# Modulation product in two matmul passes with four columns, context tiles scaled on VectorE, and a new order ahead of the first projection

## The chip, the cores and the metric

One core of one Trainium2 chip runs the whole layer as one program. The metric is the device time of one execution in microseconds (us), lower is better; the time before is the median of three executions. In the text, PE is the matmul engine (TensorE) and PEld its weight load, DVE is VectorE, ACT is ScalarE, POOL is GpSimd, and SP (SyncE) issues most of the DMAs.

## The reference, cut to what matters

The layer takes 1024 latent tokens and 256 context tokens of width 1024. Two conditioning vectors, `c` for latent tokens and `c_ctx` for context tokens, go through a SiLU and one matrix `w_mod`; the first two blocks of 1024 columns of that product are a shift and a scale for the normalised tokens. Everything else follows from the projection of the tokens so modulated.

```python
sh1, sc1, gt1, sh2, sc2, gt2 = split(silu(c) @ w_mod + b_mod, 6)        # latent tokens
sh1c, sc1c, ...              = split(silu(c_ctx) @ w_mod + b_mod, 6)    # context tokens
p  = (rms_norm(x,  norm1_g) * (1 + sc1)  + sh1)  @ w_in
pc = (rms_norm(xc, norm1_g) * (1 + sc1c) + sh1c) @ w_in
# p, pc -> differential attention and a gated delta rule, side by side
# -> output projection -> mixture of experts -> final norm
```

All of it is float32, and the kernel keeps that precision by splitting each operand into a part that the matmul takes exactly (hi, type fp32r) and the rest (lo = operand - hi).

## The kernel before

**Stages.** The program runs through modulation (to about 44 us in the profile), the projection of value and decay columns token by token (`pvab`, about 44 to 80 us), the projection of the other columns, a mix stage in which the delta rule and the attention share the engines (about 505 to 930 us), the output projection and the experts. A list scheduler orders each engine's instructions once, when the program is built; blocks marked `high_priority` are pulled ahead. On the chip each engine then runs its own list strictly in that order, and so does each DMA queue.

**Modulation** (`_modulation`). `w_mod`'s 1024 rows are taken in eight tiles of 128 rows by 2048 columns (1 MB, `wm`, three buffers, loaded through SP at L532). Before that a small chain makes the conditioning columns: a transpose to PSUM (`pv`, L546), a copy (`vec`, L547), half of it (`xh`, L553), a tanh on ACT (`th`, L554), `cs` (L555), and its hi and lo parts `csh`, `csl`. Each `wm` tile is cut into four pieces j of 512 columns. For a piece, ACT copies the hi part (`wmh`, L175), VectorE subtracts it from the original (`wml`, L176; POOL does this for j = 3 of the first six tiles), and PE adds three matmuls to one PSUM row (`mm3`, L170 to L172): csh with hi, csl with hi, csh with lo. `wmh` and `wml` have four buffers each. Two pieces of the last tile are one float32 matmul each instead (L570). A tile's buffer is loaded again, with the tile three further on, when its four subtractions are done.

**Rows to columns.** When the eighth tile is in, the two PSUM rows (2 x 2048) are copied (`mrow`, L581 and L582), transposed to 128 partitions (`pmt`, L585), and the bias is added: `mod` and `modA` are the scale, `modB` the shift (L586 to L588).

**Tokens** (`_tokens`). The two context tiles of 128 tokens come first, then latent tokens in two groups of four tiles. Per tile ACT sums the squares (`junk`, L603), VectorE makes the reciprocal root (L606 and `nt`, L148 to L163), and the tile is scaled: on ACT for the context tiles (L612), on VectorE for the latent ones (L610). PE transposes (`px`, L617), ACT writes the hi part with scale and shift (`XH`, L621), VectorE the same unrounded (`xm`, L622) and then the rest (`XL`, L623).

**First projection** (`_inproj`). Its weights come as four loads `wvr` (L390, L391), of which the last two reuse `wm` buffers and so wait for the last tiles' subtractions, and are split into `wvh` (ACT) and `wvl` (VectorE or POOL). `K.after` (L117) writes one element of a buffer on POOL so that its load waits for a chosen value: the loads of the first six latent tiles wait for `mod` this way. The `pvab` matmuls are L170 to L172 again.

**Mix** (`_mix`). The delta rule is a generator of short steps (POOL masks, PE products `p_x` L812, `p_d` L819, `p_dt` L824, VectorE `QF` L820); after every few steps the attention, 32 units of one head and one block of 128 tokens, takes its turn: scores `sp` (L1038, L1039), row maximum `mx` (L1041), exponent `pt` (L1044), combination (L1051), transposes `ptr`, products with the values `po`.

Of the kernel before, what the change touches and what calls it, by code (L numbers as in the profile page):

```python
# [367 lines left out]
def _inproj(K, banks):  # L368
# [8 lines left out]
    with tc.tile_pool(name="p1v", bufs=1, reuse_waits="tile") as pv, \  # L377
# [3 lines left out]
        with tc.tile_pool(name="p0", bufs=1, reuse_waits="tile") as pe:  # L381
            with tc.tile_pool(name="p0m", bufs=1, space=PSUM, side="right", reuse_waits="tile") as psm:
                xts, *late, raws = _modulation(K, pe, ps0, psm)
            for j in range(4):
                if j < 2:
                    wr = pv.tile([P, 2, 528], F32, name="wvr", bufs=2)
                    K.after(wr[:, 0, 0:1], late[0])
                else:
                    wr = raws.pop(0)[:, :2 * 528].rearrange("p (k f) -> p k f", k=2)
                nc.sync.dma_start(wr[:, :, 0:512], w_in[:, 2 * j:2 * j + 2, 1024:1536])  # L390
                nc.sync.dma_start(wr[:, :, 512:528], w_in[:, 2 * j:2 * j + 2, 3584:3600])  # L391
                for i in range(2):
# [132 lines left out]
def _modulation(K, pe, ps, psm):  # L525
# [19 lines left out]
    pv = ps.tile([P, 512], F32, name="pv", tag="px", bufs=3)[:, :110]  # L545
    nc.tensor.transpose(pv, vr, ident[:110, :110])  # L546
    nc.vector.tensor_copy(K.vec, pv)  # L547
    vec = K.vec
    nc.vector.tensor_scalar(K.convw, vec[:, 72:109], 0.5, None, op0=ALU.mult)
# [3 lines left out]
    nc.vector.tensor_scalar(xh, vec[:, 0:16], 0.5, None, op0=ALU.mult)  # L553
    nc.scalar.activation(th, xh, AF.Tanh)  # L554
    nc.vector.scalar_tensor_tensor(K.cs, th, 1.0, xh, op0=ALU.add, op1=ALU.mult)  # L555
    csk = K.cs.rearrange("p (w k) -> p k w", w=2)
    csh, csl = (pe.tile([P, KT, 2], F32R, name=nm) for nm in ("csh", "csl"))
    K.split(csh, csl, csk)
    pm = psm.tile([2, 2048], F32, name="pmod")
    xts, los = {}, []  # L560
    for kt in range(KT):
# [31 lines left out]
def _tokens(K, pe, ps, xts, late):  # L593
# [3 lines left out]
    for t0, n in TOKEN_GROUPS:  # L597
# [1169 lines left out]
```

## Time and profile before

| | us |
|---|---|
| three executions | 1691.02, 1693.51, 1685.58 |
| their median | 1691.02 |
| the profiled execution | 1684.6 |
| its span | 1682.8 |

| engine | busy us | share of the span |
|---|---|---|
| PE | 1536.3 | 91% |
| PEld | 1296.7 | 77% |
| DVE | 1297.9 | 77% |
| ACT | 913.7 | 54% |
| POOL | 610.7 | 36% |

The span is the time between the first and the last record of the profiled execution; 1.8 us of its own time lie around it. PE is busy nearly throughout, except at the start and in a few stretches, so a stage must be read by its own rows: the share over the whole span says nothing of the first 44 us. A timeline row gives the start, the length, the engine, the line and tile of an instruction, and in brackets how long the engine had been idle before it and what ended the wait.

### The profile page before, as it was taken

The numbers are of one execution on the slowest core, as the hardware profiler recorded it, in microseconds if no ns is written. First come the engines' busy times: TensorE is split into PE (matmuls) and PEld (weight loads), VectorE is DVE, ScalarE is ACT, GpSimd is POOL, SyncE is SP. The second block draws the span as 40 slices with busy tenths as digits, with TensorE's granted clock in tenths as the row PEclk, the third lists the DMA queues.
The fourth block names the chain that finished last, engine by engine and source line by source line (L and its number), as shares of the span: only waits on it lengthen the run. The fifth ranks groups of instructions, "written<-read, shape, count | busy, mean of one in ns | idle before, by whom it ended". The sixth has DMA issues, their size and how long they took to land.

```text
span 1682.8 us, 24852 instructions
## 1 busy us (share of the span) xinstructions
PE 1536.3 (91%) x8805; PEld 1296.7 (77%) x8805; DVE 1297.9 (77%) x2081; ACT 913.7 (54%) x1512; POOL 610.7 (36%) x555
## 2 busy tenths in 40 slices
PE   6999889899986998989899899499999999999994
PEld 2898668788876998889798788378888887777872
DVE  6757655587768777878788743799999998999985
ACT  6521125344422655656466232387777877777873
POOL 3013331232225865383640021534455333341101
PEclk9999899999997999999999999699999999999997
DMA  7477953444546031322313494799999999999965
GB/s 267 172 234 231 287 143 114 129 135 131 177 150 203 21 96 57 118 75 101 92 47 127 143 316 154 275 362 360 399 399 397 383 397 374 384 384 382 378 224 187
DMA packets 171280, 378.76 MB, mean 225 GB/s; under 512 B 32590, under 2 KB 82188, under 8 KB 170004
## 3 DMA queue, kind: packets, MB, share of 16 engines
q1 hardware_dynamic: 131874, 315.22, 51.4%
q0 software_dynamic: 12096, 45.09, 9.0%
q10 hardware_dynamic: 27186, 16.86, 4.0%
q8 instruction: 69, 1.13, 0.3%
q14 instruction: 55, 0.45, 0.1%
HBM read 316.65 MB, written 56.29 MB: 222 GB/s over the span
## 4 chain that ended last, share of the span: by engine, by line
PE 59%; DVE 11%; DMA 5%; POOL 4%; issue 3%; ACT 3%; ACTq 0%; SPq 0%; POOLq 0%; DVEq 0%
PE pgu L170 4%; PE pgu L172 4%; PE pgu L171 3%; PE pgv L171 3%; PE pgv L172 3%; PE pgv L170 3%; PE py L170 3%; PE py L171 3%; PE py L172 3%; PE po L1066 3%; PE pp L170 2%; PE pp L171 2%; PE sp L1038 2%; PE pp L172 2%; DMA qe<-eg_dram 2%
## 5 line engine op out<-in xcount | busy, mean ns | idle before, releaser
L1481 DVE TENSOR_TENSOR wlo<-raw,whi 128x1024 fp32r<-128x1024 f32 x368 | 442.3, 1242 | 23.7 <-issue 7.5
L1480 ACT ACTIVATE whi<-raw 128x1024 fp32r<-128x1024 f32 x376 | 391.7, 1063 | 99.5 <-PE pgu L171 35.1
L1428 POOL TENSOR_SCALAR onehot<-fcst,slot 128x128 bf16<-128x128 f32 x96 | 139.5, 1468 | 154.7 <-PE pls L1431 154.7
L171 PE MATMUL pl<-XH,wl 128*128 128x512 f32 x384 | 152.1, 396 | 4.4 <-DVE wl L176 4.4
L170 PE MATMUL pl<-XH,wh 128*128 128x512 f32 x384 | 152.7, 398 | 0.9 <-DVE ab L411 0.9
L172 PE MATMUL pl<-XL,wh 128*128 128x512 f32 x384 | 152.3, 397 | 0.0
L1044 ACT ACTIVATE pt<-sp,mx 128x1280 f32<-128x1280 f32 x64 | 84.9, 1326 | 56.3 <-DVE mx L1041 55.7
L1041 DVE TENSOR_REDUCE mx<-sp 128x1 f32<-128x1280 f32 x64 | 95.1, 1486 | 20.4 <-PE sp L1039 20.1
L170 PE MATMUL pgu<-whi,xTh 128*128 128x512 f32 x256 | 101.5, 397 | 5.3 <-ACT xTh L175 4.5
L172 PE MATMUL pgu<-wlo,xTh 128*128 128x512 f32 x256 | 101.5, 397 | 0.0
L172 PE MATMUL pgv<-wlo,xTh 128*128 128x512 f32 x256 | 101.2, 395 | 0.0
L171 PE MATMUL pgu<-whi,xTl 128*128 128x512 f32 x256 | 100.8, 394 | 0.0
L171 PE MATMUL pgv<-whi,xTl 128*128 128x512 f32 x256 | 100.3, 392 | 0.0
L170 PE MATMUL pgv<-whi,xTh 128*128 128x512 f32 x256 | 100.0, 391 | 0.0
L172 PE MATMUL py<-wlo,hTh 128*128 128x512 f32 x240 | 94.1, 392 | 0.9 <-DVE wlo L1481 0.9
L171 PE MATMUL py<-whi,hTl 128*128 128x512 f32 x240 | 94.1, 392 | 0.0
L170 PE MATMUL py<-whi,hTh 128*128 128x512 f32 x240 | 93.9, 391 | 0.0
L171 PEld LDWEIGHTS pl<-XH,wl 128*128 128x128 f32 x384 | 72.8, 190 | 21.2 <-DVE wl L176 5.2
L1066 PE MATMUL po<-V,aT 128*128 128x128 f32 x640 | 88.5, 276 | 0.0
L170 PEld LDWEIGHTS pl<-XH,wh 128*128 128x128 f32 x384 | 72.8, 190 | 20.2 <-issue 5.2
L1038 PE MATMUL sp<-KH,QS 128*128 128x512 f32 (+1 forms) x192 | 76.3, 397 | 12.1 <-ACT pt L1044 6.8
L172 PEld LDWEIGHTS pl<-XL,wh 128*128 128x128 f32 x384 | 72.8, 190 | 15.3 <-issue 0.9
(568 smaller groups left out, 3986.6 us busy)
## 6 DMA issues: line engine op xcount, KB each, us to landing
raw<-w_gate SPq DMA_DIRECT2D x64, 1024.0 KB
raw<-w_up SPq DMA_DIRECT2D x64, 1024.0 KB
raw<-w_down SPq DMA_DIRECT2D x64, 1024.0 KB
rwm<-w_mod POOLq DMA_DIRECT2D x32, 512.0 KB, 6.5
wr<-w_in ACTq DMA_DIRECT2D x24, 512.0 KB
wm<-w_mod SPq DMA_DIRECT2D x8, 1024.0 KB
KH<-qk_dram SPq DMA_DIRECT2D x16, 320.0 KB
xt<-x SPq DMA_DIRECT2D x8, 512.0 KB
```

The lines of the kernel that those rows point to most:

```text
L170: nc.tensor.matmul(out, ah, bh, start=start, stop=False)
L171: nc.tensor.matmul(out, al, bh, start=False, stop=False)
L172: nc.tensor.matmul(out, ah, bl, start=False, stop=stop)
L1038: nc.tensor.matmul(sp[:, k0:k1], qs, st["KH"][s][:, k0:k1], start=True, stop=False)
L1041: nc.vector.tensor_reduce(mx, sp[:, :LT], axis=AX.X, op=ALU.max, negate=True)
L1044: nc.scalar.activation(pt, sp[:, :LT], AF.Exp, bias=mx, accum_out=sm)
L1066: nc.tensor.matmul(po, aT[c], st["V"][:, c], start=c == 0, stop=c == NTT - 1)
L1428: eng.tensor_scalar(oh[:, t], iota, slot[:, t, e:e + 1], None, op0=ALU.is_equal)
L1480: nc.scalar.activation(hi, raw[:, i], AF.Copy)
L1481: eng.tensor_tensor(lo, raw[:, i], hi.bitcast(F32), ALU.subtract)
```

## The change

Six things, in the order of the diff.

1. `L394` (new): one element of `wvl` is written on VectorE from `modB` before the rests of the last weight tiles, so that those three subtractions can't be ordered ahead of `modB`.
2. The chain that makes the conditioning columns stands in a block of priority 5000, and `convw` behind it.
3. `csh` and `csl` become one tile `cs4` with four columns per row tile: two hi, two lo. The PSUM tile has four rows.
4. Each piece has two matmuls (cs4 with hi, cs4 with lo) instead of three; rows 0 and 1 gather the hi columns' product, rows 2 and 3 the lo columns'. The two halves are added after the transposes (L599, one more VectorE instruction for `mod` and one for `modB`).
5. For the first tile's pieces 0 and 1 the hi copy runs on POOL (L579) instead of ACT.
6. The context tiles are scaled on VectorE like the others.

```diff
@@ _inproj
                 nc.sync.dma_start(wr[:, :, 512:528], w_in[:, 2 * j:2 * j + 2, 3584:3600])
+                if j == 2:
+                    nc.vector.tensor_tensor(wvl[:, 4, 0:1], K.modB[:, 0, 0:1], K.modB[:, 0, 0:1], ALU.subtract)
@@ _modulation
-    pv = ps.tile([P, 512], F32, name="pv", tag="px", bufs=3)[:, :110]
-    nc.tensor.transpose(pv, vr, ident[:110, :110])
-    nc.vector.tensor_copy(K.vec, pv)
...
-    csh, csl = (pe.tile([P, KT, 2], F32R, name=nm) for nm in ("csh", "csl"))
-    K.split(csh, csl, csk)
-    pm = psm.tile([2, 2048], F32, name="pmod")
+    cs4 = pe.tile([P, KT, 4], F32R, name="cs4")
+    with tc.high_priority(5000):
+        pv = ps.tile([P, 512], F32, name="pv", tag="px", bufs=3)[:, :110]
...
+        K.split(cs4[:, :, 0:2], cs4[:, :, 2:4], csk)
+    nc.vector.tensor_scalar(K.convw, vec[:, 72:109], 0.5, None, op0=ALU.mult)
+    pm = psm.tile([4, 2048], F32, name="pmod")
...
-            K.split(hi, lo, wm[:, js], nc.gpsimd if j in QP and kt < 6 else None)
-            K.mm3(pm[:, js], csh[:, kt], csl[:, kt], hi, lo, kt == 0, kt == KT - 1)
+            if not kt and j < 2:
+                nc.gpsimd.tensor_copy(hi, wm[:, js])
+                nc.vector.tensor_tensor(lo, wm[:, js], hi.bitcast(F32), ALU.subtract)
+            else:
+                K.split(hi, lo, wm[:, js], nc.gpsimd if j in QP and kt < 6 else None)
+            nc.tensor.matmul(pm[:, js], cs4[:, kt], hi, start=kt == 0, stop=False)
+            nc.tensor.matmul(pm[:, js], cs4[:, kt], lo, start=False, stop=kt == KT - 1)
...
-                nc.tensor.transpose(pmt[:, 2 * j:2 * j + 2], mrow[:, i * D + j * P:i * D + (j + 1) * P], ident[:2, :2])
-            nc.vector.tensor_tensor(mod if i else K.modB, pmt.rearrange("p (k w) -> p k w", w=2),
-                                    vec[:, 16 + 8 * i:24 + 8 * i].unsqueeze(2).to_broadcast([P, 8, 2]), ALU.add)
+                nc.tensor.transpose(pmt[:, 4 * j:4 * j + 4], mrow[:, i * D + j * P:i * D + (j + 1) * P], ident[:4, :4])
+            pmt = pmt.rearrange("p (k r w) -> p k r w", r=2, w=2)
+            to = mod if i else K.modB
+            nc.vector.tensor_tensor(to, pmt[:, :, 0], vec[:, 16 + 8 * i:24 + 8 * i].unsqueeze(2).to_broadcast([P, 8, 2]), ALU.add)
+            nc.vector.tensor_tensor(to, pmt[:, :, 1], to, ALU.add)
@@ _tokens
-            if t0 < NT:
-                nc.vector.tensor_scalar(xs[i], xs[i], rs[:, i:i + 1], None, op0=ALU.mult)
-            else:
-                nc.scalar.activation(xs[i], xs[i], AF.Copy, scale=rs[:, i:i + 1])
+            nc.vector.tensor_scalar(xs[i], xs[i], rs[:, i:i + 1], None, op0=ALU.mult)
```

The change also moves instructions, since the scheduler orders the lists anew. On POOL at the program's start, "ISA" is, by its name in the built program, a reload of a code library; before, it stands behind the memsets, ahead of everything that waits:

```order
L1759 MEMSET const-uint8-127 128x1
L1763 UNCONDITIONAL_BRANCH
L176 ISA
L176 TENSOR_TENSOR wml<-wm,wmh 128x512
L117 COPY xt<-wml 128x1
```

and now:

```order
L1768 MEMSET const-uint8-127 128x1
L1772 UNCONDITIONAL_BRANCH
L579 CAST wmh<-wm 128x512 x2
L176 ISA
L176 TENSOR_TENSOR wml<-wm,wmh 128x512
L117 COPY xt<-wml 128x1
```

The two copies of the first tile stand ahead of it, and with them the wait for that tile.

On VectorE between the last tile's subtractions (`wml`) and the first projection's input (`XL`), before:

```order
L176 TENSOR_TENSOR wml<-wm,wmh 128x512 x2
L582 COPY mrow<-pmod 2x512 x2
L586 TENSOR_TENSOR mod<-pmt,vec 128x16
L588 SCALAR_TENSOR_TENSOR modA<-mod,vec 128x16
L176 TENSOR_TENSOR wvl<-wvr,wvh 128x528
L586 TENSOR_TENSOR modB<-pmt,vec 128x16
L622 TENSOR_SCALAR xm<-px,modA,modB 128x256
L176 TENSOR_TENSOR wvl<-wvr,wvh 128x528
L623 TENSOR_TENSOR XL_100<-xm,XH_99 128x256
```

and now:

```order
L176 TENSOR_TENSOR wml<-wm,wmh 128x512 x2
L592 COPY mrow<-pmod 4x512
L598 TENSOR_TENSOR mod<-pmt,vec 128x16
L599 TENSOR_TENSOR mod<-pmt,mod 128x16
L592 COPY mrow<-pmod 4x512
L600 SCALAR_TENSOR_TENSOR modA<-mod,vec 128x16
L598 TENSOR_TENSOR modB<-pmt,vec 128x16
L599 TENSOR_TENSOR modB<-pmt,modB 128x16
L394 TENSOR_TENSOR wvl<-modB 128x1
L176 TENSOR_TENSOR wvl<-wvr,wvh 128x528 x3
L631 TENSOR_SCALAR xm<-px,modA,modB 128x256 x2
L632 TENSOR_TENSOR XL_100<-xm,XH_99 128x256 x2
```

`modB` now stands ahead of the weights' rests, and the first `XL` behind three of them and two `xm`, where it was behind one `xm` and two rests; ACT's list likewise has all four `wvh` ahead of the first `XH`, which before stood behind two.

On PE at the start of the mix stage (delta products `p_x`, `p_d`, `p_dt`, scores `sp`), before:

```order
L1038 MATMUL sp<-KH,QS 128x512
L812 MATMUL p_x<-X,lm 128x128 x6
L819 MATMUL p_d<-X,LTm 128x128 x2
L812 MATMUL p_x<-X,lm 128x128 x4
L1039 MATMUL sp<-KL,qz_4954 128x512
L1038 MATMUL sp<-KH,QS 128x512
L1039 MATMUL sp<-KL,qz_4954 128x512
L1038 MATMUL sp<-KH,QS 128x256
L1039 MATMUL sp<-KL,qz_4954 128x256
L819 MATMUL p_d<-X,LTm 128x128 x8
L824 MATMUL p_dt<-LTm,X 128x128 x2
```

and now:

```order
L1047 MATMUL sp<-KH,QS 128x512
L821 MATMUL p_x<-X,lm 128x128 x6
L828 MATMUL p_d<-X,LTm 128x128 x2
L821 MATMUL p_x<-X,lm 128x128 x4
L828 MATMUL p_d<-X,LTm 128x128 x8
L1048 MATMUL sp<-KL,qz_4926 128x512
L1047 MATMUL sp<-KH,QS 128x512
L1048 MATMUL sp<-KL,qz_4926 128x512
L1047 MATMUL sp<-KH,QS 128x256
L1048 MATMUL sp<-KL,qz_4926 128x256
L833 MATMUL p_dt<-LTm,X 128x128 x10
```

The eight `p_d` rows moved ahead of five of the first scores (in this listing one row of `p_d` may be two matmuls on the chip). From there the two lists differ to the end of the stage: before the delta rule's last matmuls the attention is 58 of its 1056 listed matmuls further back than it was, 1.76 of its 32 units. Between modulation and mix the lists are the same.

## Rows read from the trace of the kernel before

**Rows 1.** Busy time by stretch: us, each engine's busy time (count), PE clock, DMA share, GB/s.

```profile
20.00:44.00 24.00, 20.17 (x90) 6.77 (x89) 20.84 (x35) 18.32 (x33) 11.98 (x14) 0.99 0.78 281
44.00:50.00 6.00, 4.57 (x21) 4.09 (x21) 4.39 (x10) 3.14 (x6) 1.21 (x2) 0.50 0.96 359
...
60.00:64.00 4.00, 3.02 (x25) 2.53 (x24) 2.93 (x7) 2.66 (x5) 0.00 (x0) 1.00 0.34 131
...
530.00:917.00 387.00, 354.76 (x2751) 334.82 (x2749) 307.13 (x561) 228.72 (x498) 210.87 (x221) 0.98 0.30 88
917.00:930.00 13.00, 11.32 (x87) 10.43 (x88) 8.22 (x38) 3.91 (x12) 0.00 (x0) 1.00 0.13 42
```

**Rows 2.** Timeline of VectorE, 7 to 27 us: start, length, line, tile, idle before.

```profile
7.46 0.27 DVE L547 COPY vec<-pv 128x110 f32<-128x110 f32 x1 [7.46 <-PE pv L546]
...
8.42 2.35 DVE L176 TENSOR_TENSOR wml<-wm,wmh 128x512 fp32r<-128x512 f32 x2
10.70 0.16 DVE L555 SCALAR_TENSOR_TENSOR cs<-th,xh 128x16 f32<-128x16 f32 x1
...
14.21 0.69 DVE L176 TENSOR_TENSOR wml<-wm,wmh 128x512 fp32r<-128x512 f32 x1 [2.89 <-ACT wmh L175]
...
26.56 1.25 DVE L606 TENSOR_SCALAR ms<-ss 128x2 f32<-128x2 f32 x1
```

**Rows 3.** Timeline of PE, the first modulation matmuls.

```profile
11.16 1.87 PE L170 MATMUL pmod<-wmh,csh 128*2 128x512 f32 x4 [3.73 <-ACT csh L175]
12.83 0.63 PE L171 MATMUL pmod<-wmh,csl 128*2 128x512 f32 x1
```

**Rows 4.** Tile wm: durations (ns, min/median/max) of the subtractions.

```profile
L176 DVE TENSOR_TENSOR wml<-wm,wmh x24: 678/685/1807, 7.7 to 40.1; 128x512 fp32r<-128x512 f32 x24
...
L176 POOL TENSOR_TENSOR wml<-wm,wmh x6: 1261/1304/1776, 8.9 to 29.3; 128x512 fp32r<-128x512 f32 x6
```

**Rows 5.** Timeline of ACT: the first tile's copies, `th`, the last weights' copies.

```profile
6.60 2.19 ACT L175 ACTIVATE wmh<-wm 128x512 fp32r<-128x512 f32 x4 [2.94 <-DMA wm<-w_mod]
8.69 0.20 ACT L554 ACTIVATE th<-xh 128x16 f32<-128x16 f32 x1
...
44.67 1.18 ACT L175 ACTIVATE wvh<-wvr 128x528 fp32r<-128x528 f32 x2 [0.98 <-DMA wvr<-w_in]
```

**Rows 6.** Tile xt: durations (ns) of the scaling on VectorE.

```profile
L610 DVE TENSOR_SCALAR xt<-xt,nt x4: 747/750/755, 58.8 to 60.8; 128x1024 f32<-128x1024 f32 x4
```

**Rows 7.** Timeline of VectorE, 33 to 42 us.

```profile
33.57 2.50 DVE L176 TENSOR_TENSOR wml<-wm,wmh 128x512 fp32r<-128x512 f32 x4 [0.86 <-ACT wmh L175]
...
38.35 2.41 DVE L176 TENSOR_TENSOR wml<-wm,wmh 128x512 fp32r<-128x512 f32 x2
...
41.91 0.15 DVE L586 TENSOR_TENSOR mod<-pmt,vec 128x16 f32<-128x16 f32 x1
```

**Rows 8.** Timeline of SP: issues of the first row tile, of the last weights, of the tokens.

```profile
1.57 0.41 SPq L532 DMA_DIRECT2D wm<-w_mod  x1
...
40.84 0.37 SPq L390 DMA_DIRECT2D wvr<-w_in  x1
...
42.79 11.60 SPq L521 DMA_DIRECT2D xt<-x  x6
```

**Rows 9.** Timeline of PE: the first projection's start.

```profile
46.44 0.59 PE L171 MATMUL pvab<-wvh,XL 128*128 128x264 f32 x1 [1.43 <-DVE XL L623]
```

**Rows 10.** Timeline of PE in the mix stage.

```profile
525.13 1.23 PE L824 MATMUL p_dt<-LTm,X 128*128 128x128 f32 x4 [4.00 <-DVE QF L820]
```

**Rows 11.** Mix stage by line: busy us, mean ns of one, idle before.

```profile
L1041 DVE TENSOR_REDUCE mx<-sp 128x1 f32<-128x1280 f32 x64 | 95.1, 1486 | 20.4 <-PE sp L1039 20.1
...
L1044 ACT ACTIVATE pt<-sp,mx 128x1280 f32<-128x1280 f32 x64 | 84.9, 1326 | 56.3 <-DVE mx L1041 55.7
...
L1051 DVE SCALAR_TENSOR_TENSOR pt<-pt,rt 128x1280 f32<-128x1280 f32 x32 | 60.3, 1885 | 0.7
```

**Rows 12.** Timeline of POOL at the program's start.

```profile
0.33 0.10 POOL L1759 MEMSET const-uint8-127<- 128x1 uint8 x1
8.87 1.35 POOL L176 TENSOR_TENSOR wml<-wm,wmh 128x512 fp32r<-128x512 f32 x1 [8.44 <-ACT wmh L175]
```

More of the change, by code (lines that the diff above doesn't have):

```diff
@@ L544, in _modulation @@
         r += src.shape[0]
-    pv = ps.tile([P, 512], F32, name="pv", tag="px", bufs=3)[:, :110]
-    nc.tensor.transpose(pv, vr, ident[:110, :110])
-    nc.vector.tensor_copy(K.vec, pv)
     vec = K.vec
-    nc.vector.tensor_scalar(K.convw, vec[:, 72:109], 0.5, None, op0=ALU.mult)
     xh = pe.tile([P, 16], F32, name="xh")
     th = pe.tile([P, 16], F32, name="th")
-    nc.vector.tensor_scalar(xh, vec[:, 0:16], 0.5, None, op0=ALU.mult)
-    nc.scalar.activation(th, xh, AF.Tanh)
-    nc.vector.scalar_tensor_tensor(K.cs, th, 1.0, xh, op0=ALU.add, op1=ALU.mult)
     csk = K.cs.rearrange("p (w k) -> p k w", w=2)
-    csh, csl = (pe.tile([P, KT, 2], F32R, name=nm) for nm in ("csh", "csl"))
-    K.split(csh, csl, csk)
-    pm = psm.tile([2, 2048], F32, name="pmod")
+    cs4 = pe.tile([P, KT, 4], F32R, name="cs4")
+    with tc.high_priority(5000):
+        pv = ps.tile([P, 512], F32, name="pv", tag="px", bufs=3)[:, :110]
+        nc.tensor.transpose(pv, vr, ident[:110, :110])
+        nc.vector.tensor_copy(vec, pv)
+        nc.vector.tensor_scalar(xh, vec[:, 0:16], 0.5, None, op0=ALU.mult)
+        nc.scalar.activation(th, xh, AF.Tanh)
+        nc.vector.scalar_tensor_tensor(K.cs, th, 1.0, xh, op0=ALU.add, op1=ALU.mult)
+        K.split(cs4[:, :, 0:2], cs4[:, :, 2:4], csk)
+    nc.vector.tensor_scalar(K.convw, vec[:, 72:109], 0.5, None, op0=ALU.mult)
+    pm = psm.tile([4, 2048], F32, name="pmod")
     xts, los = {}, []
@@ L569, in _modulation @@
             if j > 1 and kt == KT - 1:
-                nc.tensor.matmul(pm[:, js], csk[:, kt], wm[:, js], start=False, stop=True)
+                nc.tensor.matmul(pm[:2, js], csk[:, kt], wm[:, js], start=False, stop=True)
                 continue
             hi, lo = (pe.tile([P, 512], F32R, name=nm, bufs=WMB) for nm in ("wmh", "wml"))
-            K.split(hi, lo, wm[:, js], nc.gpsimd if j in QP and kt < 6 else None)
-            K.mm3(pm[:, js], csh[:, kt], csl[:, kt], hi, lo, kt == 0, kt == KT - 1)
+            if not kt and j < 2:
[5 more added lines that the diff above has]
+            nc.tensor.matmul(pm[:, js], cs4[:, kt], lo, start=False, stop=kt == KT - 1)
         los.append(lo.bitcast(F32)[:, 0:1])
     raws = [pe.tile([P, 2048], F32, name="wvr", tag="wm", bufs=3) for _ in range(2)]
-    mrow = pe.tile([P, 2048], F32, name="mrow", tag="wm", bufs=3)[:2]
+    mrow = pe.tile([P, 2048], F32, name="mrow", tag="wm", bufs=3)[:4]
     mod = pe.tile([P, 8, 2], F32, name="mod")
@@ L582, in _modulation @@
             nc.vector.tensor_copy(mrow[:, i * D + 512:(i + 1) * D], pm[:, i * D + 512:(i + 1) * D])
-            pmt = ps.tile([P, 512], F32, name="pmt", tag="px", bufs=3)[:, :16]
+            pmt = ps.tile([P, 512], F32, name="pmt", tag="px", bufs=3)[:, :32]
             for j in range(8):
-                nc.tensor.transpose(pmt[:, 2 * j:2 * j + 2], mrow[:, i * D + j * P:i * D + (j + 1) * P], ident[:2, :2])
-            nc.vector.tensor_tensor(mod if i else K.modB, pmt.rearrange("p (k w) -> p k w", w=2),
-                                    vec[:, 16 + 8 * i:24 + 8 * i].unsqueeze(2).to_broadcast([P, 8, 2]), ALU.add)
+                nc.tensor.transpose(pmt[:, 4 * j:4 * j + 4], mrow[:, i * D + j * P:i * D + (j + 1) * P], ident[:4, :4])
[3 more added lines that the diff above has]
+            nc.vector.tensor_tensor(to, pmt[:, :, 1], to, ALU.add)
         nc.vector.scalar_tensor_tensor(K.modA, mod, 1.0, vec[:, 64:72].unsqueeze(2).to_broadcast([P, 8, 2]),
```

## The prediction

> **What bounds the kernel now.** First the stretches [rows 1]. From 20 to 44 us, the body of the modulation, VectorE is busy 20.84 of 24 us and PE 20.17, so the shares alone don't tell which engine decides; the timeline does. VectorE's twelve subtractions of tiles 1 to 4 begin at 14.21 and the next other instruction at 26.56 [rows 2]: 12.35 us, 3.09 per tile of three, while one takes 0.685 in the median and three 2.06 [rows 4]. The missing 1.0 per tile lies in the longer ones (up to 1807 ns). VectorE runs without a gap worth naming there, so it sets the pace of the body, and PE's passes lie beside it.
>
> Not so at the start. There VectorE idles 2.89 us ahead of 14.21, for a hi copy on ACT [rows 2], and the copy waited for PE to give back one of its four buffers: PE's first modulation matmul is at 11.16, released by ACT's `csh`, and the second pass begins at 12.83 [rows 3]. PE in turn is late because `cs` was ready only at 10.86, the two subtractions at 8.42 (2.35 us) standing ahead of it [rows 2]. So the first tile ends with all of them waiting on a small chain that is badly placed.
>
> At the end of the modulation the chain is: last subtractions end at 38.35 + 2.41 = 40.76, which I call T; `mod` begins at 41.91 [rows 7]; the last weights' load is issued at 40.84 and lands for ACT at 44.67, 3.83 us on [rows 5, 8]; the token loads go out at 42.79, behind `mod` [rows 8]; and `pvab` runs in earnest from 46.44, T + 5.7, when the first `XL` is there [rows 9]. Later, in 60 to 64 us, PE is busy 3.02 of 4 [rows 1]: about 1.0 us of waiting for the latent tokens' chain. The mix stage is PE's: 354.76 of 387 us busy, 92% [rows 1].
>
> **The change part by part.** *The start (parts 2, 3, 5).* The chain now has nothing ahead of it: `vec` 7.46 to 7.73 [rows 2], then `xh`, `th`, `cs`, the hi and the lo columns, at about 0.2 each by `th` (0.20) and `cs` (0.16) [rows 2, 5], 1.0 in all with hand-overs of 0.03: about 8.8 for PE's first matmul, 2.4 earlier than 11.16. VectorE then does the first tile's three subtractions from 8.8 in 2.06 to 3.09, ending at 10.9 to 11.9, beside POOL's. The first buffers come back after two matmuls at the early spacing (12.83 - 11.16 over four, 0.42 each [rows 3]), at about 9.7, so ACT has copied a piece of tile 1 by about 10.3. Tile 1's subtractions start at about 11.5 where they started at 14.21: **-2.7 us**. The two copies moved to POOL cost between what ACT's take, 2.19 / 4 = 0.55 [rows 5], and what POOL's two-input subtraction takes, 1.30 [rows 4]; from 6.60 they end at 7.7 to 9.2, the second needed at 8.8 + 0.7 = 9.5: nothing at either end. This needs tile 1 in memory by 9.7. Its landing isn't shown, as its copies waited for PE, the first until one copy (0.6) before 14.21; at 359 GB/s [rows 1] a 1.05 MB tile takes 2.9 us after the first one's 6.60 [rows 5], 9.5. I take that, and keep a late tile 1 as a bound (no gain).
>
> *Two passes for three (parts 3, 4).* 30 matmuls of some 0.42 us leave PE, but from tile 1 on they lie behind VectorE's 3.09 per tile, so they are worth nothing more; two passes at the slow spacing would take 8 x 0.42 = 3.3 per tile, and I return to that. Pace and body stay.
>
> *Context tiles on VectorE (part 6).* Two scalings of 0.75 [rows 6] stand in VectorE's list behind tile 5's subtractions: +1.50. The 0.86 that VectorE waited there for ACT, which was scaling [rows 7], goes: net **+0.64**. T becomes 40.76 - 2.7 + 0.64 = **38.7**.
>
> *The tail (parts 1 and 4).* `mod` has one more addition of 0.15 ahead of it [rows 7]: T + 1.5 instead of T + 1.3, so the token loads go out 1.9 earlier. SP's list is the same, and POOL's `K.after` for them is behind `mod` in both. The first `XL` now stands behind more: the last weights' load is issued at T, lands at T + 3.9, the two hi copies take 1.18 [rows 5], `XH` and the rests follow, two `xm` and the `XL` on VectorE about 1.5 together. That comes to T + 7.5 against T + 5.7, so `pvab` starts at 46.2 instead of 46.44 [rows 9]: **-0.2**. What the modulation wins, the new order gives back almost whole. The three rests also stand ahead of the latent tokens' work on VectorE, but those tokens are still on their way then. The latent tokens come 1.9 earlier against a `pvab` that starts 0.2 earlier, so the 1.0 us of waiting in 60 to 64 goes: **-1.0**.
>
> *The mix (new order).* PE's busy time is the same. The eight `p_d` now run ahead of five scores, which then fill part of the 4.00 us that `p_dt` waited for `QF` [rows 10]; the attention is 1.76 units further behind at the end, where PE idled 13 - 11.32 = 1.7 us [rows 1]. The gain is at most 4.0 + 1.7 = 5.7. The loss is at most that a unit's `mx`, `pt` and combination (1.49 + 1.33 + 1.89 = 4.7 us [rows 11]) stand uncovered, 1.76 times: 8.3. At 92% busy both cancel as likely as not, and I take **0**.
>
> **The sum** is -0.2 - 1.0 = -1.2. The profiled execution would take 1684.6 - 1.2 = 1683.4. It lies 6.4 below the median of the three, 1691.0, so against that median the forecast is **1689.8**.
>
> **The rivals.** *A, slower: POOL's code reload.* Before, it could hide in the 8.44 us of POOL's idle time before its first subtraction [rows 12]. Now it stands behind the two copies, from about 7.9. Its length has no row: 0 to 8.44 by that idle time. While it runs, the first tile's fourth subtraction waits, the buffer isn't free, and tile 3's load goes out late. A load takes 6.60 - 1.57 = 5.0 us from issue [rows 5, 8], the first copy 0.55, and VectorE wants tile 3 at 11.5 + 6.2 = 17.7. So a reload of L decides from 7.9 + L + 1.3 + 5.0 + 0.6 = 17.7 on, L = 2.9, and each us beyond it is one us. At 8.44, tile 3 is 5.5 late, `pvab` starts 5.3 late, 1.0 of which the token wait gives back: front +4.3, **1695.3**. For it: the listing has it there. Against: no row shows it at work, and code may be read ahead of its place. The Trainium skill (GPSIMD Engine Reference, 2.1 Instruction dispatch) says that the first call of a freshly loaded kernel waits some 6 us for its code, measured 5.95, with no visible instruction. No row here shows or excludes it; by that figure, as an estimate, the front would be about +1.9 and the time 1692.9.
>
> *B, slower: the attention's end.* If the delay of 1.76 units stands bare, +8.3 - 1.2: **1698.1**. For it: the chain of a unit passes VectorE and ACT with nothing of its own for PE between. Against: delta work is now mixed in to the end, where before it ran alone.
>
> *C, faster.* The wait for `QF` and the idle end both go: -5.7 - 1.2, **1684.1**. For it: the order moves exactly the right rows. Against: `QF` is made on VectorE, which is busy 307 of 387 us in that stage [rows 1].
>
> *D, no gain at the start.* Tile 1 lands late, or PE stays at the slow spacing: the clock row of 44 to 50 shows 0.50, the lower of the two levels, 1.2 of 2.4 GHz [rows 1], and with a third of the passes gone PE rests more ahead of it. Then T is 40.76 + 0.64 = 41.4, or 7 tiles x (3.3 - 3.1) on top of 38.7, 40.1; `pvab` starts +2.5 or +1.2, less 1.0: up to **1692.5**.
>
> **How the numbers follow.** Chances: forecast 0.40, A 0.27, B 0.14, C 0.13, D 0.06. Nearly all cases lie within 8.45 us, 0.5% of the median, about what a measurement of this kernel can tell from no change. The forecast reaches from -3.1 (all of T's 2.1, and the 1.0) to +1 or so. The range goes from 1682, C at its bound with another 2 us for the front, to 1699, B with a little of A. Over 0.5% faster needs C with all of the front's gain, or more than I can find in the mix: 0.13. Over 0.5% slower needs A and B together or B at more than its bound: 0.12. The same: 0.75. The three executions themselves spread over 7.9 us, so the sign is best read from the profile's stages.
>
> **What the next profile should show.** First `pmod` matmul at about 8.8, tile 1's first subtraction near 11.5 (over 13: D). POOL's first subtraction right behind its copies, at 8 to 9; at 12 or later it is A, and `wm` loads would be late with it. T near 38.7, the wait of 0.86 gone. The second pass of `pvab` at about 46.2; PE in 60 to 64 with little idle time. In the mix, the wait of `p_dt` for `QF` shorter, and at its end PE no idler than before; over 5 us of new idle time there is B. The forecast is wrong if the front's net is outside -3.1 to +1, or if the mix's length changes by over 3 us either way.

## The result: slower by half a per cent, and the profile after

The changed kernel takes 1697.14 us in the median (1691.87 to 1699.54, 17 runs) beside 1688.20 (1678.86 to 1694.62, 17 runs) for the kernel before: ratio 1.0051, 95% interval [1.0036, 1.0065]. The forecast was no change, -1.2 us. The time lies inside the range, on the wrong side.

The span of the profiled execution went from 1682.8 to 1693.8 us. Some marks in the two traces say where the 11.0 us arose. T is the end of the last `wml` subtraction on VectorE; "first rx" is the first result of the other columns' projection that ACT takes from PSUM (tile `rx`); `p_oo` is the delta rule's last product, `pp` a product of the output projection; a mark is the start of the profile's row.

| mark, us from the start | before | after | difference |
|---|---|---|---|
| T | 40.76 | 34.88 | -5.9 |
| `pvab`, second pass | 46.44 | 44.65 | -1.8 |
| first rx | 129.22 | 127.75 | -1.5 |
| first score `sp` | 504.58 | 509.44 | +4.9 |
| last `p_oo` | 928.67 | 923.86 | -4.8 |
| first `pp` | 929.25 | 943.95 | +14.7 |
| last `pp` | 1047.29 | 1057.21 | +9.9 |
| span | 1682.8 | 1693.8 | +11.0 |

The front gains 1.5 us. The projection of the other columns, 375.4 us long before, takes 381.7: +6.3. From the first score to the last `p_oo` the stage is 9.7 us shorter, then 20.1 us pass where 0.6 did, and the output projection is 4.8 us shorter: together +5.1. What follows adds 1.1.

**The front.** The timeline of VectorE in the kernel after, from `vec` to `modA` (start, length, line, tile, idle before):

```profile
7.45 0.27 DVE L557 COPY vec<-pv 128x110 f32<-128x110 f32 x1 [7.45 <-PE pv L556]
...
8.22 0.96 DVE L560 SCALAR_TENSOR_TENSOR cs<-th,xh 128x16 f32<-128x16 f32 x1 [0.20 <-ACT th L559]
...
10.75 1.94 DVE L176 TENSOR_TENSOR wml<-wm,wmh 128x512 fp32r<-128x512 f32 x3
...
14.57 5.26 DVE L176 TENSOR_TENSOR wml<-wm,wmh 128x512 fp32r<-128x512 f32 x6 [0.97 <-PE pmod L584]
...
23.61 0.46 DVE L618 TENSOR_SCALAR ms<-ss 128x2 f32<-128x2 f32 x1 [0.71 <-ACT junk L615]
...
33.60 1.28 DVE L176 TENSOR_TENSOR wml<-wm,wmh 128x512 fp32r<-128x512 f32 x2
37.54 0.68 DVE L592 COPY mrow<-pmod 4x512 f32<-4x512 f32 x1 [2.66 <-ACT mrow L591]
38.72 0.17 DVE L598 TENSOR_TENSOR mod<-pmt,vec 128x16 f32<-128x16 f32 x1 [0.50 <-PE pmt L595]
38.92 0.17 DVE L599 TENSOR_TENSOR mod<-pmt,mod 128x16 f32<-128x16 f32 x1
```

Against [rows 2] and [rows 7]: the chain now goes first, tile 1's subtractions begin within the row of 10.75 (its first is tile 0's last), `ms` comes 2.95 earlier, the 0.86 wait is gone, and T is 5.9 earlier. Then VectorE stands idle ahead of `mrow`, because ACT's `mrow` waits for PE. The timeline of PE shows why:

```profile
9.78 0.58 PE L583 MATMUL pmod<-wmh,cs 128*4 128x512 f32 x1 [2.36 <-DVE cs L176]
...
26.33 0.39 PE L584 MATMUL pmod<-wml,cs 128*4 128x512 f32 x1 [1.16 <-DVE wml L176]
...
27.24 0.47 PE L583 MATMUL pmod<-wmh,cs 128*4 128x512 f32 x1
28.76 0.59 PE L584 MATMUL pmod<-wml,cs 128*4 128x512 f32 x1 [1.05 <-DVE wml L176]
29.15 0.63 PE L583 MATMUL pmod<-wmh,cs 128*4 128x512 f32 x1
29.58 0.63 PE L584 MATMUL pmod<-wml,cs 128*4 128x512 f32 x1
...
36.49 0.40 PE L584 MATMUL pmod<-wml,cs 128*4 128x512 f32 x1
...
44.65 0.57 PE L171 MATMUL pvab<-wvh,XL 128*128 128x264 f32 x1
```

From 28.76 the matmuls start some 0.43 us apart, nearly to the last one, which begins at 36.49, 1.6 after T. Of VectorE's gain of 5.9 only 3.2 reach the start of `mod` (41.91 before [rows 7], 38.72 now). And on POOL, where rival A had its code reload, the first subtraction starts 0.05 us after the copies end:

```profile
6.64 1.18 POOL L579 CAST wmh<-wm 128x512 fp32r<-128x512 f32 x2 [6.21 <-DMA wm<-w_mod]
7.87 1.27 POOL L176 TENSOR_TENSOR wml<-wm,wmh 128x512 fp32r<-128x512 f32 x1
```

**The attention's end.** The timeline of PE in the kernel after, from the delta rule's last product to the output projection:

```profile
923.86 0.39 PE L910 MATMUL p_oo<-u,AB 128*128 128x128 f32 x2
924.08 0.64 PE L943 MATMUL p_o<-ident,yo 128*128 128x128 f32 x4
929.58 1.09 PE L1069 MATMUL ptr<-ident,pt 128*128 128x128 f32 x4 [4.87 <-DVE pt L1060]
931.36 1.11 PE L1069 MATMUL ptr<-ident,pt 128*128 128x128 f32 x4 [0.69 <-ACT aT L1071]
932.27 1.91 PE L1075 MATMUL po<-V,aT 128*128 128x128 f32 x8
933.97 0.63 PE L1069 MATMUL ptr<-ident,pt 128*128 128x128 f32 x2
934.40 1.96 PE L1075 MATMUL po<-V,aT 128*128 128x128 f32 x12
936.20 0.60 PE L943 MATMUL p_o<-ident,yo 128*128 128x128 f32 x4
943.21 1.09 PE L1091 MATMUL pot<-ident,aO 128*128 128x128 f32 x4 [6.41 <-DVE aO L1088]
943.95 0.78 PE L170 MATMUL pp<-woLTN,opQS 128*128 128x512 f32 x1
```

and the same place in the kernel before:

```profile
928.67 0.39 PE L901 MATMUL p_oo<-u,AB 128*128 128x128 f32 x2
928.90 0.60 PE L1082 MATMUL pot<-ident,aO 128*128 128x128 f32 x4
929.25 0.48 PE L170 MATMUL pp<-woLTN,opQS 128*128 128x512 f32 x1
```

Before, the attention was through, but for `pot`, by the time the delta rule ended. Now its last unit stands bare: PE waits 4.87 us for the combination `pt`, 0.69 for a copy, 6.41 for the last norm `aO`, with nothing of its own between, and `pp` stands behind `pot` in PE's list. Some 6.7 us of `ptr` and `po` (1.09 + 1.11 + 0.63 + 1.91 + 1.96) have moved from ahead of the last `p_oo` to behind it.

### The profile page after: what moved, and what is told of

It is laid out like the page before. It is cut to its first block, busy times and chain, and to the rows that moved or that the text cites. A ratio compares the mean times of both kernels' runs of the same rounds, so it can differ in the third digit from the quotient of the medians.

```text
span 1693.8 us, 24798 instructions
## 1 busy us (share of the span) xinstructions
PE 1534.2 (91%) x8775; PEld 1293.9 (76%) x8775; DVE 1295.7 (76%) x2086; ACT 910.8 (54%) x1508; POOL 617.8 (36%) x557
## 4 chain that ended last, share of the span: by engine, by line
PE 55%; DVE 10%; DMA 4%; ACT 3%; issue 2%; POOL 2%; SPq 0%; POOLq 0%; ACTq 0%; DVEq 0%
PE pgu L170 3%; PE pgu L172 3%; PE pgu L171 3%; PE pgv L171 3%; PE pgv L172 3%; PE pgv L170 3%; PE py L171 3%; PE py L170 3%; PE py L172 3%; PE po L1075 2%; PE sp L1047 2%; PE pp L171 2%; PE pp L170 2%; PE pp L172 2%; DVE mx L1050 2%
## 5 line engine op out<-in xcount | busy, mean ns | idle before, releaser
L171 PEld LDWEIGHTS pl<-XH,wl 128*128 128x128 f32 x384 | 73.5, 191 | 19.5 <-DVE wl L176 3.3
L1047 PE MATMUL sp<-KH,QS 128*128 128x512 f32 (+1 forms) x192 | 75.2, 392 | 11.5 <-DVE y L511 6.3
```

The lines of the kernel that those rows point to most:

```text
L171: nc.tensor.matmul(out, al, bh, start=False, stop=False)
L1047: nc.tensor.matmul(sp[:, k0:k1], qs, st["KH"][s][:, k0:k1], start=True, stop=False)
```

## Experiments

Two theories run through the expectations. **M**: the new order of the mix, in which 20 of the attention's listed matmuls stand behind the delta rule's last `p_oo` (none before), costs the time; on the chip these 20 are the 10 `ptr` and 20 `po` of the timeline above, a listed `po` being two there. **F**: the new front costs it, through the projection stage that follows; after the first four runs it stands as **P**, the loss belongs to that stage, beside **N**, single executions differ by chance. All the marks are in a table at the end of this section, and are not told again at each run.

**A copy alone.** One needless one-element copy is added to the kernel before, on POOL, where the list of the mix stays as it was, or on VectorE, where the scheduler turns to an order with 20 matmuls behind `p_oo`.

```diff
                                        op0=ALU.add, op1=ALU.mult)
+    nc.gpsimd.tensor_copy(K.modA[:, 0, 0:1], K.modA[:, 0, 0:1])
```

```diff
                                        op0=ALU.add, op1=ALU.mult)
+    nc.vector.tensor_copy(K.modA[:, 0, 0:1], K.modA[:, 0, 0:1])
```

> The kernel before with one copy of a single element (modA onto itself) on POOL behind the modulation. The scheduler leaves the mix stage's order as before: no attention work stands behind the delta rule's last p_oo matmul. Both theories: within 2 us of before. It is the control for e2, and its profile shows how far two executions with the same order differ in the projection stage (80 to 505 us), where the changed kernel lost 5 us without a difference in its lists.

> The kernel before with the same one-element copy on VectorE instead of POOL. Its modulation is that of before, but the scheduler flips to a mix order like the changed kernel's: 20 listed attention matmuls stand behind the delta rule's last p_oo, where before there were none. Theory M (the mix order alone costs the time): 7 to 11 us slower than before, with PE's idle time of some 11 us ahead of the last transposes and of the first output projection matmul. Theory F (the front or the projection stage costs it): within 2 us of before.

Measured: with POOL's copy 1691.24 beside 1690.48, ratio 1.0004 [0.9982, 1.0026]; with VectorE's 1694.27, ratio 1.0016 [1.0000, 1.0032]. The second has the gap, 19.4 us, without any of the change: so a copy of no work brings the other order and its bare end, and a loss of 3.8 us whose interval begins at nothing. M had asked for 7 to 11, F for less than 2; neither came, so M isn't settled by it.

**Parts of the change.** The first kernel is the change without the new write of `wvl` (part 1):

```diff
-                if j == 2:
-                    nc.vector.tensor_tensor(wvl[:, 4, 0:1], K.modB[:, 0, 0:1], K.modB[:, 0, 0:1], ALU.subtract)
```

The second also takes part 6 back, which leaves the modulation alone:

```diff
-            nc.vector.tensor_scalar(xs[i], xs[i], rs[:, i:i + 1], None, op0=ALU.mult)
+            if t0 < NT:
+                nc.vector.tensor_scalar(xs[i], xs[i], rs[:, i:i + 1], None, op0=ALU.mult)
+            else:
+                nc.scalar.activation(xs[i], xs[i], AF.Copy, scale=rs[:, i:i + 1])
```

The third is the other half: the kernel before with both of these diffs the other way round, parts 1 and 6 alone.

> The changed kernel without the one-element write of the weight rests from the shift. The order of the mix is that of e2, the front almost that of the change. Theory M: faster than e2 by what the front wins, 1 to 2 us, so 6 to 9 us slower than before. Theory F: as slow as the change against before (9 us) while e2 is not.

> The changed kernel without the one-element write and with the context tiles scaled on ACT: the new modulation alone, with the mix order of e2 and e3. Theory P with the modulation's earlier end as the cause: 381 us or more for the stretch, and 5 to 8 us slower than before. If the tokens' part is the cause: like e2, 2 to 4 us slower than before.

> The kernel before with the one-element write and the context tiles on VectorE, but its own modulation with three passes: the other half, with the mix order of e2 and e3. If the modulation is the cause: like e2, 2 to 4 us slower than before and at most 380 us for the stretch. If the tokens' part is the cause: 5 to 8 us slower than before.

Measured: without the write 1697.52, ratio 1.0042 [1.0023, 1.0061]; the modulation alone 1697.89, 1.0035 [1.0014, 1.0057]; parts 1 and 6 alone 1696.09, 1.0035 [1.0015, 1.0056]. All three have the order with 20 behind, and all three are slower by 5.3 to 7.1 us, though two share no line of the change. Each of those two came out as its own expectation wanted for the part left in it as the cause, and it can't be both: that speaks for what they have in common, the order, and against any one part of the front. (Without the write M wanted a time below the one with VectorE's copy; it came 3 us above it.)

**Another share of the attention.** `UNITS` is the number of delta steps over which the 32 attention units are spread, one every 3.75 steps at 120 and every 3.4 at 108; at 108 in the changed kernel 8 listed matmuls stand behind `p_oo`.

```diff
-UNITS = 120
+UNITS = 108
```

> The changed kernel with the attention called every 3.4 delta steps instead of every 3.75 (UNITS 108 for 120). The order is the same until the 300th of the delta rule's matmuls, then the attention catches up: 8 listed attention matmuls behind the last p_oo instead of 20. Theory M with the uncovered end as the cause: faster than the change by 4 to 8 us, first output projection matmul within 5 us of the last p_oo. If the start of the mix stage were what costs: no change against the changed kernel.

Measured: 1695.81, ratio 1.0039 [1.0021, 1.0057]. M had wanted a gap under 5 us and 4 to 8 us less than the change; both were missed. The gap halves, 9.6 us, but in this profile the mix ahead of it is 12.5 us longer than in the changed kernel, as much as was freed at the end. A gap that is moved is no gain.

**A second profile of each**, with no edit, to see what one execution is worth.

> The kernel before, unchanged, for a second profile. In the first profiles the stretch from the first rotary copy (rx, 129 us) to the mix stage's first score took 375.4 us in the kernel before and 376.0 in e1, but 380.3 in e2, 385.1 in e3, 381.7 in the change and 382.1 in e4, with the same lists of instructions in it. Theory P (the loss sits in this stretch and belongs to the program): 375 to 377 again. Theory N (chance of single executions): anything from 375 to 385.

> The changed kernel, unchanged, for a second profile. Theory P: 381 to 383 us for the same stretch, and from the first score to the output projection's last matmul 547 to 549. Theory N: anything from 375 to 385.

Measured: 1691.33 and 1700.01. The projection stage of the kernel before took 383.3 us this time, 375.4 in the first profile and 376.0 with POOL's copy. So a single pair of profiles can't carry the 6.3 us: the second pair has 0.9 there (384.2 in the kernel after). Theory P falls as the whole cause; what is left of it is told below the table.

**The change's front with the other order.** The first attention unit's zero-padded query copies (`qz`) go to ACT instead of POOL. This touches nothing of the change, and the list of the mix returns to the one with none behind `p_oo`. Beside it the kernel before with the same edit.

```diff
-            nc.gpsimd.tensor_copy(padded[t % 2][rows, s], heads[h]["QS"][s][rows, t * P:(t + 1) * P])
+            if i < 1:
+                nc.scalar.activation(padded[t % 2][rows, s], heads[h]["QS"][s][rows, t * P:(t + 1) * P], AF.Copy)
+            else:
+                nc.gpsimd.tensor_copy(padded[t % 2][rows, s], heads[h]["QS"][s][rows, t * P:(t + 1) * P])
```

> The change, with one edit that touches neither the modulation nor the front: the first attention unit's zero-padded query copies go to ACT instead of POOL. With it the listing of the mix has, as in the kernel before, no attention matmul left behind the delta rule's last p_oo (the change has 20), so this is the change's front with the other order of the mix. Theory M (the order of the mix and what it uncovers at the attention's end costs the time): PE's gap between the last p_oo and the first pp, 20 us in the change, is under 2 us here, first sp to last pp lasts 538 to 552 us as in the executions of the kernel before, and since T stays at 35 to 39 and pvab starts near 45 to 46, the time is the kernel before's or up to 3 us below, 5 to 8 us below the change's. Rival F (the new front costs it, through the projection stage, whatever the mix): the gap closes as well, but the time stays 4 us or more above the kernel before, with first rx to first sp at 381 us or longer. Rival N (the gap only moves): PE idles 10 us or more elsewhere in the mix, and first sp to last pp stays at 546 to 549.

> The kernel before with the same edit, the first unit's padded query copies on ACT: the control for the run beside it. The listing of its mix is the kernel before's. All theories: within 2 us of the kernel before, gap under 2 us, T 40 to 42.

Measured: 1690.72 beside 1690.28, ratio 0.9995 [0.9979, 1.0011]; the control 1692.36, 1.0013 [0.9991, 1.0034]. The loss is gone with the gap (1.2 us). M holds; F, which wanted 4 us or more above the kernel before, falls on the time, though its mark of a projection stage of 381 us or longer is there (383.3).

**Another trigger, and the change beside it.** The same two copies on VectorE give that order too, and the change itself ran in the same rounds on the same chip.

```diff
-                nc.scalar.activation(padded[t % 2][rows, s], heads[h]["QS"][s][rows, t * P:(t + 1) * P], AF.Copy)
+                nc.vector.tensor_copy(padded[t % 2][rows, s], heads[h]["QS"][s][rows, t * P:(t + 1) * P])
```

> The change with the first unit's padded query copies on VectorE instead of ACT or POOL: another trigger for the order of the mix in which no attention matmul is listed behind the last p_oo. Theory M: gap under 2 us, first sp to last pp 538 to 552 us with a value near 544, and a time 4 to 9 us below the change in the run beside it, within 3 us of the kernel before. Rival S (what helped in the run with the copies on ACT was those copies' place, not the order): the time stays within 3 us of the change beside it although the gap is closed.

> The change itself, unedited, on the same chip and in the same rounds as the run beside it. All theories: 5 to 9 us above the kernel before (ratio 1.003 to 1.0055), gap 18 to 21 us, first sp to last pp 546 to 549 us.

Measured: with the copies on VectorE 1688.04 beside 1690.54 for the kernel before, ratio 0.9980 [0.9962, 0.9998]; the change 1699.63, ratio 1.0047 [1.0031, 1.0063]. Between these two kernels stand two small copies, and 11.6 us, more than the 4 to 9 that M gave; rival S falls. Busy time by stretch of the two (stretch, its length, each engine's busy time and count, PE clock, DMA share, GB/s), the change first:

```profile
530.00:917.00 387.00, 354.85 (x2750) 333.90 (x2749) 308.94 (x561) 224.92 (x490) 215.03 (x225) 0.98 0.31 92
917.00:945.00 28.00, 18.03 (x118) 16.25 (x116) 22.74 (x71) 12.20 (x28) 0.64 (x1) 0.87 0.18 59
945.00:1060.00 115.00, 111.46 (x573) 93.49 (x573) 48.29 (x144) 29.12 (x71) 18.41 (x14) 0.97 0.63 214
```

and with the two copies on VectorE:

```profile
530.00:917.00 387.00, 356.32 (x2769) 335.71 (x2769) 306.74 (x569) 228.56 (x498) 213.47 (x224) 0.98 0.32 94
917.00:945.00 28.00, 26.30 (x164) 22.30 (x163) 17.68 (x65) 7.20 (x20) 0.19 (x1) 1.00 0.38 114
945.00:1060.00 115.00, 104.12 (x551) 86.91 (x552) 55.35 (x170) 35.94 (x86) 23.51 (x22) 0.96 0.59 203
```

The two run alike from 530 to 917 us; from 917 to 945 PE is busy 18.0 of 28 us in the one and 26.3 in the other. PE's work at the latter's junction, where the rows of the kernel after had the gap:

```profile
930.29 0.39 PE L910 MATMUL p_oo<-u,AB 128*128 128x128 f32 x2
930.56 0.66 PE L1094 MATMUL pot<-ident,aO 128*128 128x128 f32 x4
930.97 0.48 PE L170 MATMUL pp<-woLTN,opQS 128*128 128x512 f32 x1
...
948.48 0.65 PE L170 MATMUL pp<-woh,opQS 128*128 128x512 f32 x1 [3.61 <-ACT woh L175]
```

The last row is what the gap gives back: here `pp` waits 3.61 us for the last weights' hi part, which the other order prepares in the gap; in the change none of PE's waits up to 975 us is for `woh`. The copies turn the whole order of the mix; that it is the bare end in it that costs rests on these rows.

All fourteen profiles, the two of the comparison first shown among them, in us. "Projection" is from first rx to first `sp`, "mix" from there to the last `p_oo`, "gap" from there to the first `pp`, "output" from there to the last `pp`; the column after it is the sum of those three.

| kernel | listed behind `p_oo` | T | first rx | projection | mix | gap | output | sum of three |
|---|---|---|---|---|---|---|---|---|
| before | 0 | 40.76 | 129.22 | 375.4 | 424.1 | 0.6 | 118.0 | 542.7 |
| before, again | 0 | 40.42 | 129.03 | 383.3 | 418.8 | 0.6 | 118.9 | 538.3 |
| before + POOL copy | 0 | 41.61 | 130.84 | 376.0 | 428.8 | 0.6 | 123.1 | 552.5 |
| before, first pads on ACT | 0 | 39.68 | 129.40 | 379.5 | 422.0 | 0.6 | 119.3 | 541.8 |
| before + VectorE copy | 20 | 40.83 | 130.70 | 380.3 | 413.9 | 19.4 | 112.8 | 546.2 |
| parts 1 and 6 alone | 20 | 40.72 | 130.84 | 383.3 | 416.3 | 18.3 | 112.5 | 547.1 |
| modulation alone | 20 | 39.69 | 131.00 | 385.5 | 417.2 | 18.3 | 112.8 | 548.4 |
| change without part 1 | 20 | 38.96 | 130.13 | 385.1 | 414.2 | 19.5 | 113.2 | 546.9 |
| change | 20 | 34.88 | 127.75 | 381.7 | 414.4 | 20.1 | 113.3 | 547.8 |
| change, again | 20 | 36.67 | 128.66 | 384.2 | 416.0 | 21.0 | 112.2 | 549.2 |
| change, beside the last row | 20 | 35.29 | 127.24 | 384.5 | 416.5 | 20.6 | 112.5 | 549.7 |
| change, `UNITS` 108 | 8 | 37.60 | 128.99 | 382.1 | 426.9 | 9.6 | 112.0 | 548.5 |
| change, first pads on ACT | 0 | 37.10 | 129.07 | 383.3 | 421.3 | 1.2 | 121.5 | 544.0 |
| change, first pads on VectorE | 0 | 35.40 | 127.90 | 384.2 | 418.2 | 0.7 | 118.9 | 537.8 |

Four readings.

*The order.* The sum of three is 546 to 550 wherever matmuls stand behind `p_oo`, 548.0 in the mean of eight; where none does it is 538 to 552, 542.9 in the mean of six. The 552.5 is of an execution 8.6 us above the median of its run; the other five lie at 538 to 544. What moves the sum is PE's idle time and PE's clock: take off the idle time and half of the time that the clock rows show at the lower of the two levels (an estimate: matmuls start 0.43 us apart there, 0.23 otherwise), and 472 to 477 us are left in all fourteen. Where matmuls stand behind `p_oo`, PE idles 51.7 us in the mean, for 48.2, and is at the lower level for 42.5, for 38.5; in the 552.5 it was there for 56.3. In the pair that ran side by side it differs by 11.9 us, and the spans by 12.0 (1698.1 and 1686.1).

*The front.* The change reaches first rx at 128.1 in the mean of its five profiles with `UNITS` 120 and all its parts, against 129.6 for the first four rows: -1.5.

*The projection stage.* It takes 381.7 to 385.5 in the eight profiles with the new modulation, 375.4 to 383.3 in the six with the old one, by the same lists: in the means 383.8 and 379.6, a loss of 4 us that the order of the mix doesn't explain, out of single executions that spread by 8. Where it lies can be read in the same way: in the eight PE is at the lower level for 24.4 to 31.7 us of the stage and idles 29.2 to 31.6, in the six for 13.8 to 29.3 and 24.9 to 29.5; less the idle time and half of the time at the lower level, 338 to 342 us are left in all fourteen. The two executions of the kernel before differ by the clock above all, 13.8 and 29.3 us at the lower level; their rows for this stretch, the first execution first:

```profile
129.00:500.00 371.00, 349.03 (x1832) 290.60 (x1830) 245.80 (x426) 125.72 (x303) 105.09 (x101) 0.98 0.54 164
129.00:500.00 371.00, 347.01 (x1798) 288.64 (x1797) 242.89 (x420) 123.55 (x297) 106.67 (x100) 0.96 0.53 160
```

Why PE's clock falls more often in one execution or kernel than in another, no run tried; that stays open.

*The clock.* It also divides the kernels. The granted clock of an execution, as a share of full speed, is 0.965 in the mean of the kernel before (100 executions beside the runs above) and with VectorE's copy as well; 0.964 with parts 1 and 6 alone; 0.964 and 0.963 in the change with the first pads on VectorE and on ACT; and 0.961 in the change (25 executions) and in the modulation alone. A clock lower by 0.004 over 1697 us is some 7 us of PE's time (an estimate), most of the loss of 9. By the times, the order of the mix costs 3.0 us with the old front (1694.27 beside 1691.24 with POOL's copy), at the same clock, and 11.6 with the new one, of which by the same estimate some 6 are clock (0.9605 beside 0.9640), the rest waits. Why the clock is lowest where the new modulation and the new order come together isn't shown.

## Why the prediction was wrong, by its own steps

- **The mix, the step that failed.** "At 92% busy both cancel as likely as not, and I take 0." It was +5.1 in the first pair of profiles and +11.9 in the last. The prediction's own sign of being wrong here, a mix that changes by over 3 us, was met. Of its two mechanisms the gain, rival C's, is not to be seen in the time. The wait of `p_dt` for `QF` [rows 10] did shrink in the kernel after, and stayed as it was in the kernel with VectorE's copy (second row):

```profile
526.70 1.96 PE L833 MATMUL p_dt<-LTm,X 128*128 128x128 f32 x12 [0.61 <-DVE QF L829]
531.55 0.79 PE L825 MATMUL p_dt<-LTm,X 128*128 128x128 f32 x2 [4.00 <-DVE QF L821]
```

  But the mix of the latter is the shortest in the table, 413.9 us, and the seven kernels with 20 behind have 415.5 in the mean where the six with none have 422.2: a difference of 6.7, no more than the work that was put off. Rival B did come. The step's mistake was to set gain and loss against each other by PE's share of busy time, 92% over 387 us. The wait doesn't arise in that stretch: it arises at the seam to the next stage, where PE has nothing else. The prediction gave B 8.3 us at most, by a unit's `mx`, `pt` and combination. The bare chain is longer, since behind the combination stand `ptr`, the products and the norm with its chain of small VectorE instructions, with a weight tile's multiplication (`wor`) between that chain and `aO`: 20.1 us for the gap. VectorE stood idle there for the tile's load, and the attention's norm, whose root was done at 940.15, stood behind it in the list:

```profile
941.23 1.23 DVE L763 TENSOR_TENSOR wor<-wor,gt 128x1024 f32<-128x1024 f32 x1 [1.08 <-DMA wor<-w_out]
942.38 0.68 DVE L1088 TENSOR_TENSOR aO<-aO,nt 128x512 f32<-128x512 f32 x1
```

  "Over 5 us of new idle time there is B" was the right sign, and B with its chance of 0.14 the case that came. That its time of 1698.1 lies so near to the measured 1697.14 is luck: 8.3 us for the mix stand against 5.1, and the rest is the projection stage's, which stood in no sum.
- **The loss is smaller than the gap** for a reason that the prediction didn't look for: the output projection, which before waits for its last weights, had them by then (118.0 to 113.3 us). The wait in the kernel before:

```profile
947.29 0.50 PE L170 MATMUL pp<-woh,opQS 128*128 128x512 f32 x1 [4.31 <-ACT woh L175]
```

- **The start** came as worked out: tile 1's first subtraction near 11.4 for 11.5, the first `pmod` at 9.78 for 8.8. The chain lost 0.80 in a single instruction: `cs` took 0.96 where the row it was priced by had 0.16.
- **T** was 34.9, not 38.7: "Pace and body stay" was wrong, and so was the reading under it, that VectorE runs the body without a gap worth naming. In the kernel before it waits 2.6 us there, for PE and for ACT's hi copies, most of it ahead of two rows:

```profile
17.62 2.32 DVE L176 TENSOR_TENSOR wml<-wm,wmh 128x512 fp32r<-128x512 f32 x3 [1.00 <-PE pmod L171]
...
21.09 5.54 DVE L176 TENSOR_TENSOR wml<-wm,wmh 128x512 fp32r<-128x512 f32 x6 [1.16 <-ACT wmh L175]
```

  Tiles 1 to 4 now took VectorE 11.5 us where 12.35 was taken over. From `ms` to T it was 11.3 after 14.2, a difference that is as large as what three instructions took longer in the kernel before (`ms` 1.25 for 0.46, a rest `wvl` 1.69 for 0.69, a `wml` 1.81 for 0.68); whether that is chance isn't shown. 34.9 is also the least of five executions of the new front, 35.9 their mean.
- **The tail** was "T + 1.5" for `mod` with its addition, and that ended at 39.09, T + 4.2. With two passes PE fell to the lower of its two levels: the granted clock is 0.61 from 28 to 36 us, where it was 1.00 in the first profile before, so the modulation ended with PE, not VectorE. That is the second half of rival D, without its loss. `pvab` began at 44.65 for 46.2.
- **The token wait of 1.0** did not go: PE is busy 2.89 of 4 us from 60 to 64, 3.02 before [rows 1]; its two longest waits among the tokens, 0.65 and 0.34 us before, are 0.71 and 0.33, with one of 0.50 besides.
- **The front's net** was thus -1.5 for -1.2, right in size by errors that cancel: a better T, a worse tail, a token wait that stayed. That the sum fits is luck.
- **Rival A** did not happen: POOL's first subtraction follows its copies by 0.05 us. The figure of some 6 us that the Trainium skill (GPSIMD Engine Reference, 2.1 Instruction dispatch) gives for a first call is not borne out at this place; whether the code had come in during the 6.21 us of waiting ahead of the copies, no row shows.
- **What stood outside the sum**: the projection stage, counted at nothing as its lists are the same, was 6.3 longer in the first pair of profiles, 0.9 in the second, 4 in the means of all. PE's clock, which the sum took as it was but for rival D at the front, fell from 0.965 to 0.961 over the whole execution, an estimated 7 us.

The change with the first unit's copies on VectorE is the version to keep: 0.9980 [0.9962, 0.9998] of the kernel before, a gain that barely clears the noise and that its sister with the copies on ACT (0.9995) doesn't show. What in the scheduler turns the order over on so little wasn't tried.

## What to carry to other kernels

When an edit reorders a long overlapped stage, don't price the order by the stage's busy share: look at which chain is last at its seam, follow that chain to its very end, and ask what the engine has to do meanwhile. A list scheduler can turn a stage over on an edit of no weight, so compare the lists of both kernels beyond the edited code, and run the edit together with a second, weightless one that brings the old order back, before you judge the edit itself. One profile of each kernel isn't enough where executions differ by as much as the effect: here a stage with the same lists moved by 8 us between two of the same kernel, most of it PE's clock, so set the granted clock beside every time that you compare.

## What the runs showed of the hardware

With fewer passes PE was slower where it mattered. Busy time by stretch, 28 to 36 us, before:

```profile
28.00:36.00 8.00, 5.58 (x24) 1.59 (x22) 6.81 (x18) 6.41 (x11) 1.26 (x1) 1.00 0.83 322
```

and after:

```profile
28.00:36.00 8.00, 7.18 (x16) 1.36 (x17) 6.88 (x12) 4.44 (x8) 4.44 (x2) 0.61 0.68 220
```

Sixteen matmuls take longer than twenty-four did: the granted clock went from 2.4 to 1.2 GHz, its other level. It did so before the wait of 1.05 us at 28.76, for the matmul at 27.24 already takes 0.47 us where its like take 0.40; what PE had done until then was to wait 0.51, 0.29 and 1.16 us between 23.6 and 26.3. The length of one wait doesn't tell: in the kernel before a longer one left the clock at 1.00.

```profile
31.56 0.40 PE L172 MATMUL pmod<-wml,csh 128*2 128x512 f32 x1 [2.41 <-DVE wml L176]
```

Between 28 and 36 us executions differ, 0.58 to 0.79 with the new modulation and 0.79 to 1.00 with the old one; over 20 to 44 us the clock is 0.79 to 0.84 in the eight profiles with the new modulation and 0.93 to 1.00 in the six with the old one. Which of the modulation's parts does it was not tried. The same comes behind the gap at the attention's end: after 6.41 us of idle time the first `pp` start some 0.43 us apart, until 949.13, and 0.23 from there on:

```profile
948.36 0.63 PE L171 MATMUL pp<-woKN,oppt 128*128 128x512 f32 x1
948.79 0.50 PE L172 MATMUL pp<-woLTm,opQS 128*128 128x512 f32 x1
949.13 0.39 PE L170 MATMUL pp<-woWT,opQS 128*128 128x512 f32 x1
949.36 0.39 PE L171 MATMUL pp<-woWT,oppt 128*128 128x512 f32 x1
```

Twelve matmuls at 0.2 us more each are 2.4 us of the gap's price that no wait shows. The kernel before pays some 1.4 of the same kind: behind its 4.31 us at 947.29, `pp` start 0.43 us apart from 948.45 to 951.43.

The other surprise: single instructions that lasted 0.8 to 3 us beyond their like. In the kernel after `cs` took 0.96 for 0.16, a step of the reciprocal root at 26.87 took 1.24 for 0.16, and one of POOL's three `wvl` rests 4.39 us:

```profile
L176 POOL TENSOR_TENSOR wvl<-wvr,wvh x3: 1305/1312/4389, 31.6 to 40.0; 128x528 fp32r<-128x528 f32 x3
```

They stand in the stretch in which the weights come in; that it is the loads that hold them was not tried.
